# A hybrid decoder step on one core: the attention's masked products move to VectorE, the gate projection's pieces and the sample's state units change places, and one normalisation starts a piece later

## The chip, the cores and the metric

The kernel runs on one core of one Trainium2 chip. The metric is the device time of one execution in microseconds (us), as the median of several runs. TensorE (PE in the profile) multiplies matrices, VectorE (DVE), ScalarE (ACT) and GpSimd (POOL) do elementwise work, and SyncE (SP) issues the DMAs. Each engine works through its own queue in order; the engines wait for each other by semaphores. TensorE writes its results to PSUM, which this kernel uses as eight banks of 512 float32 values per partition. All operands of GpSimd in this kernel are in SBUF.

## The reference

One layer of a decoder is computed for a prompt of 1024 tokens and a sample group of 8 sequences of 4 tokens, in float32, with a width of 1024:

```
h = RMSNorm(x);  proj = h @ w_in
z | x,B,C | dt | q | k | v = split(proj)
y_ssd = RMSNorm( (SSD scan of silu(conv4(x,B,C)), dt) * silu(z) )      # 8 heads x 64, state 128, chunks of 128
y_att = sliding-window attention(q, k, v), window 128                  # 8 heads x 64, 2 kv heads, sinks, ALiBi
x = x + concat(y_ssd, y_att) @ w_out
h = RMSNorm(x);  u = conv3(h @ w_up);  x = x + (silu(u_gate) * u_val) @ w_down
```

The outputs are both groups' x, the last states of the scan and of the two convolutions, and the last keys and values.

## The kernel before, in words

The 1056 tokens (1024 of the prompt, then 32 of the sample) lie along the free dimension, features on the partitions. A float32 product is made of three passes: each operand is split into a rounded high part and a remainder, and `dense` (L147) issues high x high, high x low and low x high for each block of 128 inputs.

**Attention** (`att_unit`, L495 to L531) runs once for each of 8 query blocks and 2 halves of the heads, 16 times. TensorE makes the scores (L503), `probs` turns them into probabilities on VectorE, ScalarE and GpSimd, and TensorE transposes these into one PSUM bank `pt` (L517). The window of a block covers two key blocks, and the probabilities of both are held in one matrix: the entries on one side of the diagonal belong to the block's own keys, the others to the block before. So ScalarE copies the whole transposed matrix to SBUF (L519, `pt_[:, 1]`), GpSimd multiplies that copy by the triangle `tri` (L520, `pt_[:, 0]`), and TensorE multiplies both with values (L525): the masked part with the difference of the two value blocks (`vdif`), the whole with the values of the block before (`vall`). ScalarE copies the result out (`ya`, L530), and a DMA stores it to `yatt`.

**The state stage** follows a list of steps, `PLAN`. Each step issues the instructions of one piece:

- `uGT` is `ssd_unit`: the state unit of head group G (0 or 1) and token block T (0 to 7; 8 is the sample). It transposes its operands into a `px` bank (L611), scales them on GpSimd (`xd`, L618, L619), multiplies in banks `yy` (L653, L655), and updates the state that the next unit carries on, through the only bank of tag `st` (L660, L667). Decay rows are broadcast by DMA (`ab<-acd`, `Cs<-ead`). The sample's unit keeps its own result in the bank of tag `st` (L673, L684), loads four pieces of the old state (`h0`, `h<-in_h0T` in the profile), and makes masks and products on GpSimd (`cm`, L676; L643).
- `x0M` is `xbc`: one of the eight 128-wide chunks of the x,B,C projection with its convolution (L261 to L275).
- `zGI` is `z_block`: the gate projection of group G for token block I of the three blocks 0 to 384, 384 to 768 and 768 to 1056, that is 2 x 24 matmuls of 384 or 288 columns, and its silu (L708 to L710).
- `nGI` is `gate_norm`, the gated norm of a block (L719 to L739); `a0I` loads a block of the attention's output and splits it into the output projection's operands; `sGI` splits the state stage's result the same way.
- `oMQ` is `out_piece`: 24 matmuls for 128 output features M and quarter Q of the tokens (264 columns). Quarters 0 and 1 need token blocks 0 and 1 alone.

The operands of the output projection reuse the memory of the operands x of the input projections, so they can be written when the last gate piece has read x.

**After the plan** the loop at L939 issues the pieces of quarters 0 and 1 that the plan left out, with `half_done` after each M, which squares the result and adds it to a sum (`ssum`, L846). `half_prep(0)` then makes the norm of the first half: sums over the partitions on TensorE (L851), a reciprocal root on VectorE, a broadcast on TensorE (L858), the scaled result (L870), and the operands of the up projection (L882 to L887). The loop at L945 issues the pieces of quarters 2 and 3, in the order M = 4, 5, 6, 7, 0, 1, 2, 3. The up projection (L988) follows in a seven-product scheme, and then the down projection (L147).

The order of the instructions on each engine is not the program's alone: the framework lays it out when the kernel is built, with the program's order as priority and by times that it estimates, and lets later work go ahead where earlier work is not ready by its estimate.

## Time and profile before

| | |
|---|---|
| median of 3 runs | 1208.59 us (1203.76 to 1208.68) |
| profiled execution | 1208.17 us, its span 1206.4 us |
| TensorE busy | 1161.6 us, 96% |
| VectorE busy | 866.0 us, 72% |
| ScalarE busy | 506.6 us, 42% |
| GpSimd busy | 345.7 us, 29% |
| mean granted clock of TensorE | 0.98 |

A row of the timeline gives the start in us from the span's start, the duration, the engine, the line, the operation with what it writes and reads, and in brackets how long the engine sat idle before it and what it waited for. A row of the table by stage gives the stretch, its length, the busy time of each engine with the number of instructions, the mean granted clock of TensorE (1.00 is full, the clock is at full or half), the share of the DMA engines and their rate. In the list of waits, `A <- B: us, times, longest` says that A waited for B.

### The profile page before, as it was taken

The page shows a single profiled execution, that of the slowest core. Times are in us where ns is not written, and L with a number is a line of the kernel's source. Part 1 is how long each engine was busy: PE and PEld are TensorE (multiplying, and loading weights), DVE is VectorE, ACT ScalarE, POOL GpSimd, SP SyncE. Part 2 cuts the span into 40 slices and gives each one's busy share as a digit, 9 for nine tenths or more (in the row PEclk, how much of TensorE's full clock was granted, in tenths as well). Part 3 has the DMA queues.
Part 4 walks back from the last instruction along what each step waited for, and adds up shares of the span by engine and source line. Part 5 has one row for each costly group of instructions (what it writes and reads, how often), then busy time and mean ns, then how long its engine had stood idle before and what let it go on. Part 6 is the DMA issues. An engine that isn't in the chain of part 4 may idle for free.

```text
span 1206.4 us, 22111 instructions
## 1 busy us (share of the span) xinstructions
PE 1161.6 (96%) x8614; PEld 1112.8 (92%) x8614; DVE 866.0 (72%) x1739; ACT 506.6 (42%) x992; POOL 345.7 (29%) x471
## 2 busy tenths in 40 slices
PE   7999999989989999888999999999999999999998
PEld 7998878869867999888999999999999999999998
DVE  7678857476686677897766676666666787777764
ACT  7444643444544344464545454545544322112110
POOL 0125445253444000044344343534343111001000
PEclk9999999999988899899999999999999999999999
DMA  8211112132645413113222222222222854323303
GB/s 291 63 62 57 36 32 75 29 84 79 184 144 164 169 71 131 43 54 106 87 75 81 80 72 80 72 80 71 89 72 89 336 174 145 121 89 119 102 9 145
DMA packets 52362, 122.53 MB, mean 102 GB/s; under 512 B 9233, under 2 KB 19985, under 8 KB 52241
## 3 DMA queue, kind: packets, MB, share of 16 engines
q1 hardware_dynamic: 52256, 121.12, 29.9%
q8 instruction: 67, 1.10, 0.4%
q14 instruction: 39, 0.31, 0.1%
HBM read 94.86 MB, written 27.26 MB: 101 GB/s over the span
## 4 chain that ended last, share of the span: by engine, by line
PE 82%; DVE 8%; DMA 5%; ACT 2%; issue 2%; POOL 1%; SPq 0%; POOLq 0%; DVEq 0%; ACTq 0%
PE ps L147 37%; PE ps L988 31%; PE ps L199 6%; DMA raw<-in_wup 2%; DVE au L935 1%; PE ps L525 1%; PE sc L503 1%; PE yy L653 1%; DVE x2l L883 1%; PE ps L517 1%; PE st L660 1%; DMA Cs<-ead 1%; DVE c L1030 1%; DMA xr<-in_xT 1%; PE ps L339 0%
## 5 line engine op out<-in xcount | busy, mean ns | idle before, releaser
L988 PE MATMUL ps<-x2h,au 128*128 128x264 f32 x2464 | 456.4, 286 | 10.6 <-ACT x2h L882 4.0
L988 PEld LDWEIGHTS ps<-x2h,au 128*128 128x128 f32 x2464 | 384.0, 189 | 13.2 <-ACT x2h L882 4.4
L988 PE MATMUL ps<-x2l,au 128*128 128x264 f32 x1232 | 348.8, 285 | 0.4 <-DVE x2l L883 0.4
L988 PEld LDWEIGHTS ps<-x2l,au 128*128 128x128 f32 x1232 | 232.5, 189 | 0.8 <-DVE x2l L883 0.8
L1103 DVE TENSOR_TENSOR acc<-acc,ps 128x352 f32<-128x352 f32 x264 | 131.1, 517 | 65.3 <-PE ps L147 64.7
L147 PE MATMUL ps<-xh,uh 128*128 128x264 f32 (+3 forms) x528 | 163.8, 318 | 10.1 <-ACT xh L182 5.6
L147 PE MATMUL ps<-gh,ul 128*128 128x352 f32 x528 | 170.1, 322 | 0.0
L147 PE MATMUL ps<-gl,uh 128*128 128x352 f32 x528 | 170.0, 322 | 0.0
L147 PE MATMUL ps<-gh,uh 128*128 128x352 f32 x528 | 167.9, 322 | 0.6 <-ACT gh L179 0.6
L147 PE MATMUL ps<-xl,uh 128*128 128x264 f32 (+3 forms) x528 | 166.2, 315 | 0.3 <-DVE xl L183 0.3
L147 PE MATMUL ps<-xh,ul 128*128 128x264 f32 (+3 forms) x528 | 165.4, 313 | 0.0
L116 ACT ACTIVATE uh<-raw 128x1024 fp32r<-128x1024 f32 (+3 forms) x59 | 55.9, 953 | 194.1 <-PE ps L147 173.7
L1030 DVE SCALAR_TENSOR_TENSOR c<-u,colt,c 128x1072 f32<-128x1072 f32 x88 | 119.9, 1364 | 3.6 <-ACT c L1028 3.5
L147 PEld LDWEIGHTS ps<-xh,uh 128*128 128x128 f32 x528 | 101.5, 195 | 14.5 <-ACT xh L182 6.6
L935 DVE TENSOR_TENSOR au<-raw,au 128x512 fp32r<-128x512 f32 x115 | 78.7, 700 | 39.9 <-ACT au L934 39.8
L147 PEld LDWEIGHTS ps<-xl,uh 128*128 128x128 f32 x528 | 102.8, 195 | 1.8 <-DVE xl L183 0.8
L147 PEld LDWEIGHTS ps<-xh,ul 128*128 128x128 f32 x528 | 102.8, 195 | 1.8 <-issue 1.0
L147 PEld LDWEIGHTS ps<-gh,uh 128*128 128x128 f32 x528 | 98.8, 188 | 0.9 <-ACT gh L179 0.9
L147 PEld LDWEIGHTS ps<-gl,uh 128*128 128x128 f32 x528 | 99.2, 188 | 0.4
L147 PEld LDWEIGHTS ps<-gh,ul 128*128 128x128 f32 x528 | 99.3, 188 | 0.0
L934 ACT ACTIVATE au<-raw 128x512 fp32r<-128x512 f32 x115 | 71.2, 625 | 34.8 <-PE ps L147 9.0
L935 DVE TENSOR_TENSOR au<-t,au 128x512 fp32r<-128x512 f32 x46 | 41.6, 904 | 36.0 <-PE ps L988 18.9
(295 smaller groups left out, 1936.8 us busy)
## 6 DMA issues: line engine op xcount, KB each, us to landing
raw<-in_wup SPq DMA_DIRECT2D x46, 512.0 KB, 3.6
gr<-gd SPq DMA_DIRECT2D x22, 528.0 KB, 4.8
gd<-c SPq DMA_DIRECT2D x22, 512.0 KB, 2.6
raw<-in_wdn SPq DMA_DIRECT2D x22, 512.0 KB, 4.1
raw<-in_wout SPq DMA_DIRECT2D x12, 512.0 KB, 3.5
acc<-in_xT SPq DMA_DIRECT2D x16, 264.0 KB, 5.3
accd<-acc SPq DMA_DIRECT2D x16, 264.0 KB, 2.1
acc<-accd SPq DMA_DIRECT2D x8, 528.0 KB, 8.2
```

Of the source, the lines that this page charges most:

```text
L116: act.activation(out=hi, in_=raw, func=AF.Copy)
L147: pe.matmul(out=ps, lhsT=w(a, k), rhs=x(b, k), start=first and k == ks[0] and i == 0, stop=last and k == ks[-1] and i == 2)
L199: pe.matmul(out=ps[:m, :n], lhsT=x[k][c][:, a:a + m], rhs=w[k // nk][b][:, o:o + n], start=k == 0 and i == 0, stop=k == 7 and i == 2)
L503: pe.matmul(out=sb[:, v, c].rearrange("p i k -> p (i k)"), lhsT=qT[a][r, c], rhs=kT[b][r, o:o + 256], start=i == 0, stop=i == 2)
L517: pe.transpose(out=pt[:, h], in_=P[:, h], identity=ident)
L525: pe.matmul(out=po[64 * v:64 * v + 64, 0:256].rearrange("p (c q) -> p c q", c=2), lhsT=(vall[:, t - i] if i or not t else vdif[:, t - 1])[ ...
L653: pe.matmul(out=o, lhsT=xw[:, c], rhs=M[:, 2 * i + h], start=True, stop=not off)
L934: act.activation(out=u[:, 0:512], in_=src, func=AF.Copy)
L935: dve.tensor_tensor(out=u[:, 512:1024], in0=src, in1=u[:, 0:512].bitcast(F32), op=ALU.subtract)
L988: pe.matmul(out=ps, lhsT=wgt[:, 512 * a + 128 * k:512 * a + 128 * k + 128], rhs=xx[b][:, k], start=opens and k == 0 and i == 0, stop=k == ...
L1030: dve.scalar_tensor_tensor(out=c[:, 0:n], in0=u[:, j:j + n], scalar=col(C_FW + 3 * m + j), in1=c[:, 0:n], op0=ALU.mult, op1=ALU.add)
L1103: dve.tensor_tensor(out=o, in0=o, in1=ps[:, :PC], op=ALU.add)
```

## The change

It has three parts.

1. The masked product of an attention block (L520) runs on VectorE, and reads the transposed probabilities in PSUM in place of ScalarE's copy in SBUF.
2. `PLAN` is another order of the same steps. The sample's unit u08 comes after u11 and no longer after u04; z11 and z12 come between u10, u11, u08 and u12 and no longer ahead of u10; u18 comes after o21 near the end and no longer after n02; n02, s02, s11, s01 and the output pieces among them change places.
3. `half_prep(0)` is issued after the first piece of the second half (M = 4, quarter 2) and no longer ahead of it.

```
-PLAN = """u00 x07 u01 z00 u02 x06 x05 u03 u04 u08 u05 z01 u06 z10 u07 n00 z02 n01 z11 z12 u10 u11 u12 a00 u13 s00 n10 u14 s10 n02 u18 s02 u15 o20 o10 n11 s11 a01 u16 a02 o00 o30 u17 n12 s01 o21 o31 s12"""
+PLAN = """u00 x07 u01 z00 u02 x06 x05 u03 u04 u05 z01 u06 z10 u07 n00 z02 n01 u10 z11 u11 u08 z12 u12 a00 u13 s00 n10 u14 n02 s10 u15 o20 s02 n11 o10 a01 u16 s11 s01 o00 u17 a02 o30 o21 u18 n12 o31 s12"""
...
             pt_ = p.tile([128, 2, 4, 128], F32, tag="pt", name="pt", bufs=2)
             act.activation(out=pt_[:, 1], in_=pt, func=AF.Copy)
-            pool.tensor_tensor(out=pt_[:, 0], in0=pt_[:, 1], in1=b3(tri.unsqueeze(1), 128, 4, 128), op=ALU.mult)
+            dve.tensor_tensor(out=pt_[:, 0], in0=pt, in1=b3(tri.unsqueeze(1), 128, 4, 128), op=ALU.mult)
...
         half_done(m, 0, m == 0)
-    half_prep(0)
     for i, m in enumerate((4, 5, 6, 7, 0, 1, 2, 3)):
         if i >= 4:
             w[m] = None
         for q in (2, 3):
             out_piece(m, q)
+            if i == 0 and q == 2:
+                half_prep(0)
         half_done(m, 1, i == 0)
```

## The prediction

> **What bounds the kernel now.** I read the busy shares first, then the chain that ended last, then a table of busy times by stage, and only then the waits inside the stages that the change touches.

> ```profile
> span 1206.4 us, 22111 instructions
> PE 1161.6 (96%) x8614; PEld 1112.8 (92%) x8614; DVE 866.0 (72%) x1739; ACT 506.6 (42%) x992; POOL 345.7 (29%) x471
> PE 82%; DVE 8%; DMA 5%; ACT 2%; issue 2%; POOL 1%; SPq 0%; POOLq 0%; DVEq 0%; ACTq 0%
> ...
> core 0: us, PE busy (x) PEld busy (x) DVE busy (x) ACT busy (x) POOL busy (x), PEclk, DMA share, GB/s
> 105.00:265.00 160.00, 153.88 (x1123) 132.72 (x1125) 107.84 (x338) 75.61 (x226) 70.19 (x85) 0.98 0.16 47
> 265.00:329.50 64.50, 61.47 (x438) 54.06 (x434) 46.00 (x104) 36.04 (x87) 25.51 (x38) 0.95 0.44 133
> 329.50:403.50 74.00, 64.47 (x443) 53.09 (x443) 59.60 (x167) 31.07 (x77) 29.52 (x41) 0.82 0.49 146
> 403.50:430.70 27.20, 25.21 (x211) 25.00 (x212) 12.56 (x22) 7.26 (x11) 0.00 (x0) 1.00 0.47 163
> 430.70:478.00 47.30, 47.30 (x392) 47.30 (x392) 40.94 (x78) 20.73 (x33) 0.40 (x4) 1.00 0.27 97
> 478.00:572.50 94.50, 83.50 (x649) 80.60 (x647) 78.28 (x129) 48.98 (x87) 26.72 (x35) 0.96 0.21 73
> 572.50:945.00 372.50, 372.50 (x3053) 372.50 (x3054) 250.23 (x381) 187.22 (x328) 150.58 (x215) 1.00 0.25 83
> ```

> TensorE bounds the whole. From 572.50 us on it has no idle time, so whatever is won or lost before arrives at the end in full. What an edit can win is TensorE idle time and a low granted clock. The stages are attention (105 to 265), the first state units with gate pieces beside them (265 to 329.5), the later state units with output pieces (329.5 to 403.5), the rest of the first half's output pieces (to 430.7) and the second half's (to 478). The third is the poorest: 74.00 - 64.47 = 9.5 us idle, and a mean clock of 0.82, which costs up to 0.18 x 74 = 13.3 us, 22.9 us in all. Attention has 160.00 - 153.88 = 6.1 us idle.

> **Part 1, the masked product.** Removed are 16 products on POOL, each behind ACT's copy of the transposed probabilities; added are 16 on VectorE that read the same PSUM bank.

> ```profile
> L520 POOL TENSOR_TENSOR pt<-pt,cs x16: 1260/1290/2364, 108.7 to 262.1; 128x512 f32<-128x512 f32 x16
> ...
> PE ps L525 <- POOL pt L520: 3.1, 3, 2.1
> PE ps L147 <- DVE u L261: 1.8, 2, 1.5
> ...
> 162.91 1.08 PE L525 MATMUL ps<-pt,vdif 128*64 128x256 f32 x4 [2.08 <-POOL pt L520]
> ...
> L180 DVE TENSOR_TENSOR kTl<-ps,kTh x3: 173/677/684, 80.1 to 81.7; 128x512 fp32r<-128x512 f32 x2, 128x32 fp32r<-128x32 f32 x1
> ...
> 60.41 0.23 DVE L363 SCALAR_TENSOR_TENSOR dtr<-ps,rstd,rowt 128x8 f32<-128x8 f32 x1 [2.71 <-ACT vall L362]
> ```

> The trace has no such product on VectorE. The nearest row is L180: one operand from PSUM, one from SBUF, 512 columns, 0.68 us. So VectorE takes 16 x 0.68 = 10.9 us more, 107.84 to 118.7 us in 160. L363 shows that VectorE waits for ACT's last read of a PSUM tile, though it reads nothing that ACT wrote, so I let the product start after ACT's copy, as POOL's did. A block's latency then falls by 1.29 - 0.68 = 0.6 us, not by the whole 1.29. [...]

> Only three of the sixteen products kept TensorE waiting (3.1 us); the others are covered by projection matmuls of L147. At 162.91 0.6 of the 2.08 us goes, of the second (3.1 - 2.08 - 0.55) its 0.5. The third, the last block, is worth most:

> ```profile
> 259.72 2.41 POOL L119 TENSOR_TENSOR ul<-raw,uh 128x1024 fp32r<-128x1024 f32 x1
> 262.09 2.31 POOL L520 TENSOR_TENSOR pt<-pt,cs 128x512 f32<-128x512 f32 x1
> ...
> 261.34 5.58 DVE L270 SCALAR_TENSOR_TENSOR c<-u,chalf,c 128x1080 f32<-128x1080 f32 x3 [2.00 <-ACT c L267]
> ...
> 264.45 0.65 PE L525 MATMUL ps<-pt,vdif 128*64 128x256 f32 x4 [0.55 <-POOL pt L520]
> ...
> 268.57 1.17 PE L638 MATMUL px<-fm 128*128 128x128 f32 x4 [1.69 <-ACT xt L614]
> 270.89 1.22 PE L660 MATMUL st<-xd,xt 128*128 128x256 f32 x2 [1.15 <-POOL xd L619]
> ```

> The product waits on POOL behind a weight split and ends at 264.40, while VectorE idles for 2 us until 261.34. On VectorE it can end near 261, three microseconds earlier, and the output copy, its DMA and the first state unit behind them follow. The 0.55 goes, of the next two gaps (2.84 us) I take half, 1.4, and half of the clock loss in 265 to 329.5 (0.05 x 64.5 = 3.2), 1.6. Against that stands VectorE's longer queue (the convolution of L261 and L270 is behind it, and TensorE waits for L261 already 1.8 us): +0.6. Sum: -0.6 - 0.5 - 0.55 - 1.4 - 1.6 + 0.6 = **-4**. Ends: -11 (the 3.1 and 2.84 us and all clock loss of both stages, 0.02 x 160 + 3.2, with a little over for VectorE), and +2 (three exposed products each behind one L270, 1.3 us, in place of the 0.6 won).

> **Part 2, the order of the steps.** No work is added. The sample's unit of the first group (u08) goes from after u04 to after u11, past five units; that of the second (u18) from after u14 to after u17, past three; z11 and z12 go between u10, u11, u08 and u12; the splits s11 and s01 go ahead of o00.

> ```profile
> 329.50:354.00 24.50, 19.49 (x132) 15.06 (x134) 22.13 (x50) 13.16 (x36) 11.20 (x14) 0.79 0.54 157
> 354.00:382.00 28.00, 26.22 (x187) 20.87 (x181) 20.97 (x63) 11.22 (x28) 11.99 (x20) 0.82 0.42 118
> 389.50:402.50 13.00, 10.26 (x62) 9.30 (x61) 10.78 (x37) 4.47 (x7) 0.61 (x1) 0.74 0.41 151
> 300.00:321.00 21.00, 21.00 (x147) 17.79 (x146) 12.64 (x30) 9.37 (x24) 8.86 (x14) 1.00 0.66 208
> ...
> 307.03 0.65 PE L673 MATMUL yy<-xd,ab 32*128 32x64 f32 x4
> ...
> 323.80 0.68 PE L660 MATMUL st<-xd,xt 128*128 128x256 f32 x2
> ...
> 1133.70 22.97 PE ps L147 x144
> ...
> h<-in_h0T SPq DMA_DIRECT2D x16, 256.0 KB, 4.2
> Cs<-ead SPq DMA_DIRECT2D x14, 256.0 KB, 3.6
> ```

> Four terms. (i) 389.5 to 402.5 is the end of the plan, where o21 waits for the last splits: 13.00 - 10.26 = 2.7 us idle and 0.26 x 13 = 3.4 of clock. With s01 early, o21, o31 and ten more output pieces that need no third block can run beside u18 and the last norm. A piece is 24 matmuls of the 392 that took 47.30 us, so 2.9 us, and ten are 29 us of cover. Two thirds of 6.1: -4. (ii) 354 to 382 is u18 now: 1.8 idle and 0.18 x 28 = 5.0 of clock. At the end it has that cover: -4. Here the clock falls while TensorE is busy 26.22 of 28 us, with 32-wide matmuls (L673, L684). [...] (iii) u08 sits now at 300 to 321, where TensorE has 21.00 of 21 us of work at full clock, so it costs nothing. In its new place z12 covers it. A 352-column matmul takes 22.97 / 144 = 0.16 us, so z12's 48 of 288 columns are 6.3 us and z11's of 384 are 8.4 us. I give it most of what u18 costs where it is now: +5. (iv) z11 and z12 leave 303 to 328 and come in among u10 to u12, where 329.5 to 354 loses 5.0 idle and 0.21 x 24.5 = 5.1 of clock; two units are done sooner: -2. Sum: **-5**.

> Every instruction of u08 and u18 moves with them: per unit four loads of 256 KB on SP (4.2 us each to landing), two stores and a broadcast, and on POOL three copies, two scalings, the mask and four products. On SP u08's now stand behind the broadcasts of u05 to u11 (3.6 us each) and ahead of those of u12, u18's behind the loads of a01 and a02 and the weights of o00 to o21; I cost that at nothing, since two buffers of each let the loads run ahead, and in (iii) where they do not. Output pieces wait for x to be free, that is for z12: the attention load a00 and its POOL splits come after it as before. Ends of the part: -22.9, the stage's whole loss, and +15.5, priced below.

> **Part 3, the norm sums one piece later.**

> ```profile
> 429.60 0.55 PE L851 MATMUL ps<-ones,ssum 128*88 128x1 f32 x5 [1.99 <-DVE ssum L846]
> ...
> 478.18 0.43 DVE L777 TENSOR_TENSOR acc<-acc,ps 128x264 f32<-128x264 f32 x1 [2.51 <-PE ps L147]
> ```

> The 1.99 us in which TensorE waits for the sum are filled by o42 (2.9 us): **-2**. The normalisation on VectorE begins 2.9 - 2.0 = 0.9 us later while the pieces end 2 us earlier. VectorE idles 2.5 us before the last piece's addition, so its work still ends in time. Late next is the second half's normalisation, which follows the last piece and moves with it. Ends: -2 and +1.

> **Sum**: 1208.2 us, the time of the profiled execution (span 1206.4), - 4 - 5 - 2 = 1197. The three runs shown have a median 0.4 us above it, 1208.59, and one of 1203.76; I let 1197 stand against either.

> **Rivals.** *The state bank (slower).* u08 holds the single bank of tag st, in which each unit makes its state update, from 307.03 until the next update at 323.80: 16.8 us, in which no following unit can hand on its state. Now z02, z11 and z12 fill that. After u11 only z12 is sure, 6.3 us, so 10.5 us lie open, with the clock loss of u18's window, 5.0, beside them, and the output pieces start later, so that (i), (ii) and (iv) do not come: part 2 is +15.5 and the time 1208.2 - 4 - 2 + 15.5 = 1218. It decides for slower when over 7 us of the hold lie open. For it: 329.5 to 354 has VectorE at 22.13 of 24.50 already. Against: a unit's y needs the state before, not the bank, so u12, its norm and the first output pieces can run in the hold. 14%. *No change.* The product is hidden anyway, as thirteen of sixteen are; u08 inherits what u18 paid; only part 3 comes: 1206. For it: TensorE is 96% busy. Against: the idle time at the plan's end has a cause that the order removes. 24%. *More.* Dense pieces beside all units keep the clock up and three quarters of the 22.9 us go, -17: 1208.2 - 4 - 17 - 2 = 1185. For it: 300 to 321, the same kind of unit with dense pieces beside it, runs at clock 1.00. Against: the dense work is the same in total. 12%. My forecast, 1190 to 1203, has the other 50%.

> **Numbers.** About 0.5%, 6 us, is what a measurement of this kernel can tell from no change. Faster: 0.50 + 0.12, less a little for the forecast's upper edge, 0.60; slower 0.14; the rest 0.26. The range leaves out the deepest gain and the worst of the state bank: 1184 to 1212; the forecast's own is 1190 to 1203.

> **What would show it.** Part 1: a product row on VectorE near 0.68 us, behind ACT's copy; no wait of L525 for POOL; state units from 262 us on. Part 2: clock over 0.9 between the plan's gate pieces and its end, no idle time before the last o21 piece; wrong if the next state update after u08 comes over 10 us late with TensorE idle. Part 3: L851 without idle time ahead of it, and the products of the up projection starting 2 us nearer to it. The instruction order of each engine is laid out by a planner from estimated times; if it places far more than the edited steps otherwise, the sum by terms is void.

## The result, and the profile after

The changed kernel takes 1192.66 us (median of 6 runs, 1190.98 to 1195.53) against 1206.97 us (6 runs): ratio 0.9888, 95% interval 0.9871 to 0.9905, or 14.3 us less. The prediction said 1197.0 in 1184 to 1212. The profiled execution took 1193.78 us. Medians and ratios here and below leave out three executions with a low granted clock: one of the kernel before, one of h4_last, and the profiled one of f1_mask_head, whose mean clock was 0.535 over a span of 2168.7 us, so its trace is not used.

First the page's busy line, then the busy times by stage; the stages are those of the prediction's table, moved to where the matching work now stands. The new order also moves work between them: the second row has 486 matmuls for 438 before, the third 387 for 443.

```profile
span 1192.0 us, 22098 instructions
PE 1150.6 (97%) x8614; PEld 1108.3 (93%) x8614; DVE 872.0 (73%) x1755; ACT 504.7 (42%) x992; POOL 316.6 (27%) x455
PE 86%; DVE 9%; ACT 2%; issue 2%; DMA 1%; POOL 0%; SPq 0%; ACTq 0%; DVEq 0%
```

```profile
core 0: us, PE busy (x) PEld busy (x) DVE busy (x) ACT busy (x) POOL busy (x), PEclk, DMA share, GB/s
105.00:263.20 158.20, 155.02 (x1134) 134.12 (x1135) 112.30 (x355) 75.87 (x227) 44.44 (x70) 0.99 0.15 47
263.20:330.80 67.60, 65.20 (x486) 58.85 (x486) 52.93 (x125) 37.83 (x93) 27.77 (x42) 0.95 0.43 134
330.80:391.50 60.70, 48.43 (x387) 41.23 (x387) 50.77 (x144) 27.93 (x70) 25.79 (x36) 0.94 0.51 168
391.50:417.00 25.50, 25.50 (x211) 25.29 (x211) 12.06 (x24) 6.98 (x11) 0.00 (x0) 1.00 0.50 167
417.00:464.00 47.00, 47.00 (x394) 47.00 (x393) 37.77 (x73) 19.66 (x31) 0.40 (x4) 1.00 0.26 92
```

The one line to see is TensorE's busy time. The same 8614 matmuls took 1161.6 us before and take 1150.6 now: 11.0 of the span's 14.4 us are matmuls that run faster, and only 3.4 are idle time (1206.4 - 1161.6 = 44.8 before, 41.4 now). In the stage with the late state units, the clock was 0.82 and is 0.94, while TensorE idles longer there than before: 60.70 - 48.43 = 12.3 us, where 329.50 to 403.50 had 9.5. In these two traces the change won clock more than idle time.

That holds over all runs, not only in this trace. Each run lists its span and its mean granted clock; clock times span is called its time at full clock here, and the rest is what the clock took. The means over the runs, each ratio against the runs of the kernel before that were made beside it:

| kernel | parts in it | median us | ratio, 95% interval | at full clock | lost to the clock |
|---|---|---|---|---|---|
| before (86 runs) | none | 1207.0 | 1 | 1181.6 | 23.5 |
| changed | all three | 1192.7 | 0.9888 [0.9871, 0.9905] | 1180.1 | 10.9 |
| e1_mask | mask product | 1205.0 | 0.9981 [0.9963, 0.9999] | 1182.0 | 21.3 |
| e2_plan | order | 1209.4 | 1.0029 [1.0011, 1.0047] | 1184.1 | 24.3 |
| e3_norm | norm sums | 1204.3 | 0.9974 [0.9961, 0.9988] | 1181.9 | 20.0 |
| e4_mask_plan | mask, order | 1196.0 | 0.9908 [0.9889, 0.9927] | 1179.3 | 14.7 |
| f1_mask_head | mask, order up to u14 | 1200.8 | 0.9949 [0.9934, 0.9965] | 1179.1 | 20.4 |
| f2_mask_tail | mask, order from u14 | 1205.4 | 0.9988 [0.9973, 1.0003] | 1184.4 | 18.9 |
| h1_last_plan | last product, order | 1210.0 | 1.0031 [1.0006, 1.0057] | 1184.9 | 23.0 |
| h2_g0_plan | group 0's products, order | 1204.9 | 0.9990 [0.9974, 1.0006] | 1180.6 | 22.8 |
| h4_last | last product | 1207.5 | 0.9994 [0.9974, 1.0014] | 1181.2 | 23.1 |
| g2b_bank | mask, order, other bank | 1207.9 | 1.0014 [1.0001, 1.0027] | 1185.0 | 21.0 |
| f4_copy_plan | mask from SBUF, order | 1193.7 | 0.9898 [0.9878, 0.9919] | 1178.6 | 13.5 |
| h3_after_copy | all three, mask from SBUF | 1189.0 | 0.9856 [0.9834, 0.9878] | 1178.4 | 9.2 |

The last two columns add up to the span, which is 1.8 us short of the time. Their standard errors are 0.2 and 0.4 us for the kernel before, 0.4 to 1.1 and 0.6 to 2.0 for the others. By this split 12.6 of the changed kernel's 14.3 us are clock and 1.5 time at full clock. The two parts are not independent: over the 86 runs of the kernel before, an execution that lost 1 us more to the clock had 0.47 us less time at full clock (a fitted line), so it took only 0.53 us longer. The split says where the time stands, not what each us of clock is worth. A single execution of the kernel before scatters by 3.8 us (standard deviation) in what the clock takes, so a single trace says little about differences of 3 us; what follows leans on medians, and on traces for where things stand.

### The profile page after: what moved, and what is told of

Same layout as the page of the kernel before. It is cut to its first block, busy times and chain, and to the rows that moved or that the text cites. A ratio compares the mean times of both kernels' runs of the same rounds, so it can differ in the third digit from the quotient of the medians.

```text
span 1192.0 us, 22098 instructions
## 1 busy us (share of the span) xinstructions
PE 1150.6 (97%) x8614; PEld 1108.3 (93%) x8614; DVE 872.0 (73%) x1755; ACT 504.7 (42%) x992; POOL 316.6 (27%) x455
## 4 chain that ended last, share of the span: by engine, by line
PE 86%; DVE 9%; ACT 2%; issue 2%; DMA 1%; POOL 0%; SPq 0%; ACTq 0%; DVEq 0%
PE ps L147 39%; PE ps L989 32%; PE ps L199 6%; PE ps L525 1%; PE sc L503 1%; DVE au L935 1%; DVE x2l L883 1%; PE two L147 1%; DVE c L1031 1%; DMA raw<-in_wup 1%; PE ps L517 1%; PE yy L653 1%; PE st L660 0%; DMA gr<-gd 0%; PE px L611 0%
## 5 line engine op out<-in xcount | busy, mean ns | idle before, releaser
L147 PE MATMUL ps<-xh,uh 128*128 128x264 f32 (+3 forms) x528 | 164.1, 317 | 8.8 <-ACT xh L182 5.8
L147 PE MATMUL ps<-gh,ul 128*128 128x352 f32 x528 | 170.1, 322 | 0.0
L147 PE MATMUL ps<-gl,uh 128*128 128x352 f32 x528 | 170.0, 322 | 0.0
L147 PE MATMUL ps<-gh,uh 128*128 128x352 f32 x528 | 167.9, 322 | 1.1 <-ACT gh L179 1.1
L147 PE MATMUL ps<-xl,uh 128*128 128x264 f32 (+3 forms) x528 | 165.6, 314 | 0.0
L147 PE MATMUL ps<-xh,ul 128*128 128x264 f32 (+3 forms) x528 | 165.1, 313 | 0.0
L147 PEld LDWEIGHTS ps<-xh,uh 128*128 128x128 f32 x528 | 101.3, 193 | 12.6 <-ACT xh L182 5.8
L147 PEld LDWEIGHTS ps<-xl,uh 128*128 128x128 f32 x528 | 102.1, 193 | 1.8 <-POOL xl L180 0.4
L147 PEld LDWEIGHTS ps<-xh,ul 128*128 128x128 f32 x528 | 102.1, 193 | 1.5 <-issue 0.8
L147 PEld LDWEIGHTS ps<-gh,uh 128*128 128x128 f32 x528 | 98.8, 188 | 1.3 <-ACT gh L179 1.3
L147 PEld LDWEIGHTS ps<-gl,uh 128*128 128x128 f32 x528 | 99.2, 188 | 0.4
L147 PEld LDWEIGHTS ps<-gh,ul 128*128 128x128 f32 x528 | 99.3, 188 | 0.0
L119 DVE TENSOR_TENSOR ul<-raw,uh 128x1024 fp32r<-128x1024 f32 (+3 forms) x51 | 62.3, 1231 | 10.8 <-ACT uh L116 10.8
```

The costliest lines, as they stand in the source:

```text
L119: (e or dve).tensor_tensor(out=lo[:, i:i + n], in0=raw[:, i:i + n], in1=hi[:, i:i + n].bitcast(F32), op=ALU.subtract)
L147: pe.matmul(out=ps, lhsT=w(a, k), rhs=x(b, k), start=first and k == ks[0] and i == 0, stop=last and k == ks[-1] and i == 2)
```

## The experiments

**One part at a time.** e1_mask has the product on VectorE and nothing else, e2_plan the new PLAN alone, e3_norm the moved call of half_prep alone, e4_mask_plan the first two.

```
e1, e4:  -pool.tensor_tensor(out=pt_[:, 0], in0=pt_[:, 1], ...)
         +dve.tensor_tensor(out=pt_[:, 0], in0=pt, ...)
e2, e4:  -PLAN = """... u04 u08 u05 ... z11 z12 u10 u11 u12 ... u14 s10 n02 u18 s02 ...
         +PLAN = """... u04 u05 ... u10 z11 u11 u08 z12 u12 ... u17 a02 o30 o21 u18 ...
e3:      -half_prep(0) ahead of the loop
         +half_prep(0) after o42
```

> Part 1 alone: the masked product on VectorE, the plan and the place of the norm as before. Theory A (the prediction's terms add up: each part takes away a wait of its own): -4 us against the kernel before, ratio about 0.997; the last L525 about 7 us earlier than at 265.16 as in the changed kernel, of which some 3 us arrive at the first state unit. Rival B (the parts only pay together: the new plan is fitted to the block's new latency, and the planner's order of fillers moves): 0 to +3 us, ratio 1.000 to 1.003. Rival C (the plan carries nearly all): 0 us.

> Part 2 alone: the new order of steps, the product still on GpSimd. Theory A: the changed kernel is 14 us faster, 2 of them from part 3 and 4 from part 1, so -8 us, ratio 0.993; granted clock of 0.94 between the last gate piece and the end of the plan as in the changed kernel, in place of 0.82. Rival B: -4 us or less, ratio over 0.997. Rival C: -12 us, ratio 0.990.

> Part 3 alone: the first half's norm sums after piece o42. Theory A: -2.0 us, ratio 0.9983, L851 with no idle time before it, the first product of the up projection 2 us earlier and the wait at the second half's norm (498 to 503 us before) as long as it was. Rival: VectorE is late by 0.9 us more and gives part of it back there: -1 us.

> Parts 1 and 2, without part 3. Theory A: 2 us slower than the changed kernel, -12 us against before, ratio 0.990, and equal to the sum of the runs of part 1 alone and part 2 alone within 2 us. Rival B: much more than that sum, by 5 us or over. Rival C: equal to part 2 alone.

Against 1207.0 the mask alone gives -2, the norm sums alone -2.7, the order alone +2.4 with an interval that excludes a gain, and mask and order together -11. The terms do not add: the mask and the order sum to about 0, and 11 us come only when both are there. Rival B's reading (they pay together) stands, though its 0 to +3 us for the mask alone was not met; Theory A and Rival C fall. The norm sums add up by the time, 1196.0 - 1192.7 = 3.3 us on top of the two; how they do is taken up further below.

The profiled executions of the order alone (span 1209.3 us) and of mask and order (1195.3 us) differ by 14.0 us. Half of that, 7.0 us, lies at the end of the plan; 3.3 are won before the first state unit (266.56 and 263.24 us) and the rest in smaller parts. The first row is the order alone, the second mask and order, both the stretch between the second sample unit and the last o21; the matmul count is the same.

```profile
388.20:409.00 20.80, 17.23 (x99) 16.04 (x97) 15.39 (x41) 8.84 (x14) 0.00 (x0) 0.76 0.52 178
```

```profile
383.20:397.00 13.80, 12.50 (x99) 11.80 (x98) 11.50 (x33) 6.63 (x10) 0.00 (x0) 1.00 0.66 226
```

The same 99 matmuls take 20.80 us at clock 0.76 or 13.80 at 1.00, with 3.6 and 1.3 us idle. The 5.0 us of clock in this are one execution's: the changed kernel, with the same new order, has 0.87 at this place in its trace (further below). The chain of TensorE's waits in these parts (371 to 410 and 366.8 to 400 us):

```profile
PE ps L147 <- ACT xh L179: 1.5, 1, 1.5
PE ps L147 <- ACT uh L116: 0.7, 1, 0.7
PE ps L147 <- DVE xl L180: 0.5, 1, 0.5
PE ps L147 <- DVE ul L119: 0.5, 1, 0.5
PE nb L737 <- DVE yms L140: 0.3, 1, 0.3
```

```profile
PE ps L147 <- ACT xh L179: 1.3, 1, 1.3
```

With the order alone TensorE waits for splits of x and of the output weights four times close together; with the mask too, once.

**Head or tail of the order.** Both runs have the mask product on VectorE. f1_mask_head takes the new order up to u14, f2_mask_tail from there on.

```
f1:  ... u04 u05 z01 ... u10 z11 u11 u08 z12 u12 ... | u14 s10 n02 u18 s02 u15 ... (old)
f2:  ... u04 u08 u05 ... z11 z12 u10 u11 u12 ... (old) | u14 n02 s10 u15 ... o21 u18 n12 o31 s12
```

> The mask on VectorE, and of the new order only its head (z11 and z12 between u10 and u12, u08 after u11); from u14 on the old order, with u18 after s10 and the early splits late. Measured so far: mask alone 1205.0, mask with the whole new order 1196.0 us. Theory A (the tail, u18 last and the splits ahead, carries what the order saves once the mask is on VectorE; the head only costs u08's hold of the state bank): no gain from the head, 1204 to 1209, and the next state update after the group's last stands still behind u18. Rival B (the head carries it: the state units of the first group come sooner): 1197 to 1201. Rival C (only the whole order pays, since the planner lays out each half badly): 1203 to 1208 here and in the run with the tail alone.

> The mask on VectorE, the old head (u08 after u04, z11 and z12 ahead of u10), and the new tail (n02 ahead of s10, s11 and s01 ahead of o00, u18 last). Theory A (the tail carries the gain): 1193 to 1198, at or below the 1196.0 of mask with the whole new order, since u08 holds the state bank at a place where other work fills it. Rival B (the head carries it): 1202 to 1206, the mask alone being 1205.0. Rival C (only the whole pays): 1203 to 1208.

On top of the mask's 1205.0 the head gives -4.2, the tail +0.4, both -9.0. The head wins 2.9 us at full clock (1182.0 to 1179.1); the tail by itself loses 2.4 there. After the head the tail costs nothing at full clock (1179.3) and takes 5.7 us off the clock's loss. So Rival B's ranges were met (Rival C's only in f2), Theory A falls, and the tail pays only behind the new head.

**Is it the last block's late product?** In the prediction the last of the sixteen products carried most of part 1. h4_last moves only that one, h1_last_plan the same under the new order; every other instruction keeps its place on its engine. h2_g0_plan moves the eight of group 0 and leaves the last one on POOL.

```
+dv = g == 1 and t == 7          (h1, h4)      +dv = g == 0          (h2)
+(dve if dv else pool).tensor_tensor(out=pt_[:, 0], in0=pt if dv else pt_[:, 1], ...)
```

> The new order with only the last of the sixteen masked products (group 1, query block 7) on VectorE, the other fifteen on POOL as before. The order of the instructions on TensorE, ScalarE and SyncE is that of the new order alone (1209.4 us); only this product changes its queue. Theory A (the new order alone loses because the last product waits on POOL behind a weight split, which makes the first state unit 3 us late, and that alone undoes what the order saves): 1198 to 1203. Rival B (the late product is worth its own delay and no more): 1206 to 1208. Rival C (the gain of both parts together comes from where the planner puts the instructions once it counts the products on VectorE): 1206 to 1210, the state stage unchanged.

> The new order with the eight masked products of group 0 on VectorE and the eight of group 1, the late last one among them, on POOL. The planner then lays out the state stage nearly as with all sixteen on VectorE (the state updates stand at the same places among the gate projection's matmuls up to the tenth). Theory A (the last product's lateness undoes the gain): 1205 to 1210. Rival B (a product is worth its delay): about 1208. Rival C (the layout carries it): 1195 to 1200, with the first half's output pieces ending below 419 us.

> The kernel before with only the last masked product on VectorE; the order of every other instruction is unchanged. Theory A (most of what the mask is worth is the last block, as the prediction put it: its gap, half of the next two, and half of the clock loss behind them): 1204 to 1206, as the mask alone, the first state unit 2 to 3 us sooner. Rival B (it is the other fifteen, or the layout that follows from them): 1206 to 1208, that is nothing that can be told from the 1207.0 of before.

Under the new order Theory A falls: 1210.0 us where it said 1198 to 1203, beside 1209.4 with no product moved. Under the old order nothing can be told (1207.5 against 1207.2 beside it): the interval, 0.9974 to 1.0014, leaves room for a gain of 3 us and so for Theory A's 1204 to 1206. The timeline decides more. First h1_last_plan, below it the rows of e2_plan.

```profile
260.36 0.69 DVE L520 TENSOR_TENSOR pt<-ps,cs 128x512 f32<-128x512 f32 x1 [0.82 <-ACT pt L519]
264.03 0.65 PE L525 MATMUL ps<-pt,vdif 128*64 128x256 f32 x4
265.58 0.87 PE L611 MATMUL px<-idt,fm 128*128 128x128 f32 x6
```

```profile
265.01 0.65 PE L525 MATMUL ps<-pt,vdif 128*64 128x256 f32 x4 [0.55 <-POOL pt L520]
266.56 0.87 PE L611 MATMUL px<-idt,fm 128*128 128x128 f32 x6
```

The product ends at 261.05, as the prediction had it, but TensorE reaches its user only at 264.03, without waiting: other matmuls stand ahead of it in TensorE's order. h4_last shows the same under the old order; its rows, and below them the one of the kernel before that goes with the prediction's:

```profile
256.15 0.60 PE L517 MATMUL ps<-idt,s 128*128 128x128 f32 x4
257.76 0.69 DVE L520 TENSOR_TENSOR pt<-ps,cs 128x512 f32<-128x512 f32 x1 [0.82 <-ACT pt L519]
261.43 0.65 PE L525 MATMUL ps<-pt,vdif 128*64 128x256 f32 x4
265.29 0.87 PE L638 MATMUL px<-fm 128*128 128x128 f32 x4 [1.43 <-ACT xt L614]
267.87 1.22 PE L660 MATMUL st<-xd,xt 128*128 128x256 f32 x2 [1.72 <-POOL xd L619]
```

```profile
258.55 0.60 PE L517 MATMUL ps<-idt,s 128*128 128x128 f32 x4
```

From the transposes (L517) to the product's user (L525) TensorE needs 261.43 - 256.15 = 5.28 us, before 264.45 - 258.55 = 5.90. So the earlier product is worth 0.6 us to TensorE and not three, and the two gaps behind it are 1.43 + 1.72 = 3.15 us where they were 2.84. (The state units start at 262.98 in this trace, 3.0 us sooner than before; 1.7 of that is one half-rate stretch less ahead of them.) With all sixteen on VectorE the planner draws the attention's products forward (the last L525 of the changed kernel starts at 257.9 us):

```profile
L525 PE MATMUL ps<-pt,vall x64: 379/379/430, 112.1 to 257.9; 128*64 128x256 f32 x64
```

With group 0 alone the state units are laid out almost as in e4_mask_plan, and full-clock time drops to 1180.6. But the clock still takes 22.8 us, and between 386 and 404 us, at the plan's end, TensorE still waits for a split (first row). Its last product is not late, though it is still on POOL (the rows below): the planner has put POOL's weight split behind it, it ends at 259.53, and TensorE takes it up at 261.70 without waiting.

```profile
PE ps L147 <- ACT uh L116: 2.9, 1, 2.9
```

```profile
258.25 1.28 POOL L520 TENSOR_TENSOR pt<-pt,cs 128x512 f32<-128x512 f32 x1 [5.42 <-ACT pt L519]
261.70 0.65 PE L525 MATMUL ps<-pt,vdif 128*64 128x256 f32 x4
262.79 2.40 POOL L119 TENSOR_TENSOR ul<-raw,uh 128x1024 fp32r<-128x1024 f32 x1
```

At 1204.9 us it is 4.5 us below the order alone, and still above Rival C's 1195 to 1200. Theory A's number (1205 to 1210) is nearly met, but its reason, a late last product, is absent; so this run does not test it. With h1, though, the delay of the last product is excluded as the cause of the 11 us, and h4's rows say why. What is left is the order that the planner makes when it counts all sixteen on VectorE, together with the latency of the other fifteen. These two could not be separated, since any other subset moves the order as well; that the differing waits are for splits over 100 us behind the products speaks for the order, but it is an argument and no run shows it alone.

**Does u08's hold of the state bank cost?** g2b_bank puts the sample units' y and its transpose into tag nb, under mask and order.

```
-yy = psd.tile([128, 512], F32, tag="st" if smp else "yy", name="yy")
+yy = psd.tile([128, 512], F32, tag="nb" if smp else "yy", name="yy")
-ps = psd.tile([128, 512], F32, tag="st", name="yt")
+ps = psd.tile([128, 512], F32, tag="nb", name="yt")
```

> Mask on VectorE and the new order (1196.0 us), and the sample units' y and its transpose in the bank of tag nb, so that u08 no longer holds the single bank of tag st. Theory A (u08's hold, 13.8 us from its first product to the next state update with some 4.6 us of it idle, is what the new order still pays): 1191 to 1194, the next state update within 8 us of the one before. Rival B (the hold is covered, the idle time there comes from VectorE's queue): 1195 to 1197. Rival C (the norm's sums, which use nb, now wait for the sample units): 1197 to 1202.

It is 12 us slower than e4_mask_plan, outside all three. The hold did not cost what Theory A said: with the bank free the next state update after u08's first product at 327 comes at 339.25 (first row), in the changed kernel at 340.93 (the rows below it).

```profile
339.25 0.70 PE L660 MATMUL st<-xd,xt 128*128 128x256 f32 x2
```

```profile
327.16 0.88 PE L673 MATMUL yy<-xd,ab 32*128 32x64 f32 x6
339.68 0.41 PE L691 MATMUL yt<-idt,ys 128*128 128x128 f32 x2 [0.71 <-DVE ys L688]
340.93 0.67 PE L660 MATMUL st<-xd,xt 128*128 128x256 f32 x2 [0.51 <-DVE fm L698]
```

TensorE's longest waits in g2b_bank, from 326 to 424 us, show what came in its place:

```profile
PE px L611 <- DVE cb L640: 3.1, 1, 3.1
PE nb L737 <- DVE yms L140: 2.6, 2, 1.4
PE ps L147 <- DVE ul L119: 1.6, 1, 1.6
```

The long gap for cb stays (3.4 us in the changed kernel), so it comes from VectorE, which in the changed kernel is busy for all of 331.29 to 334.70, and not from the bank. The norm's L737 in nb now waits 2.6 us where it did not wait in e4_mask_plan, but for VectorE's `yms`, not for the sample unit; the wait for the bank that Rival C named is seen only the other way round, with 0.4 us before the sample unit's L673. The planner has put that second sample unit behind the norm, at 385 us where it was at 368. Since the order moved too, the 12 us are not the price of the bank alone.

**Where the product reads from.** f4_copy_plan (on e4_mask_plan) and h3_after_copy (on the changed kernel) read ScalarE's copy in SBUF; all engines keep their order.

```
-dve.tensor_tensor(out=pt_[:, 0], in0=pt, ...)
+dve.tensor_tensor(out=pt_[:, 0], in0=pt_[:, 1], ...)
```

> Mask on VectorE and the new order, as in the run of both (1196.0 us), but VectorE's product reads the copy that ScalarE has made in SBUF, not the PSUM bank. The instructions stand in the same order on every engine. Theory A (the product waits for ScalarE's read of the bank in any case, so where its operand lies is nothing): 1195 to 1197, the product's row 0.6 to 0.75 us. Rival B (two SBUF operands make VectorE share with POOL, as other such products show 0.16 us alone and 0.93 beside a POOL operation): the row is uneven, some of the sixteen over 1 us, and the time 1197 to 1201.

> The changed kernel whole, with its masked product on VectorE reading ScalarE's copy in SBUF in place of the PSUM bank; the instructions stand in the same order on every engine. In the run with the first two parts the same edit gave 1193.7 against 1196.0 us, which their intervals do not tell apart. Theory A (where the operand lies changes nothing, since the product waits for ScalarE in any case and the row was 0.68 us there as well or near it): 1191 to 1194, with the 1192.7 of the changed kernel inside. Rival B (a product that reads SBUF is shorter or frees the PSUM bank sooner, and the 2.3 us repeat): 1189 to 1191, faster than both kernels. By the split of each run into its time at full clock and what the clock took, mean granted clock times span: A 1179 to 1181 at full clock, 10 to 13 lost.

The first row is the changed kernel's product, the second h3_after_copy's (shortest, median and longest duration in ns).

```profile
L520 DVE TENSOR_TENSOR pt<-ps,cs x16: 678/692/692, 108.3 to 253.6; 128x512 f32<-128x512 f32 x16
```

```profile
L520 DVE TENSOR_TENSOR pt<-pt,cs x16: 678/692/1829, 107.7 to 252.4; 128x512 f32<-128x512 f32 x16
```

Both times are lower, by 2.3 and 3.6 us, but neither pair's intervals part (0.9889 to 0.9927 and 0.9878 to 0.9919; 0.9871 to 0.9905 and 0.9834 to 0.9878). h3_after_copy's 1189.0 us (4 runs) is the lowest of all and below both kernels; that it beats the kernel before is shown, that it beats the changed one is likely and not shown. The row is no shorter, and one product of the sixteen takes 1.83 us: it starts 1.11 us into a weight split of POOL (L119), and outlasts it. Operations of POOL that start while such a product runs are longer too: L325 takes 0.57 us for 0.20 in the changed kernel, L492 1.53 to 1.55 for 1.04. In the changed kernel, with the operand in PSUM, a product also starts 1.11 us into a split of L119 (243.68 in 242.57 to 244.96 us) and takes 0.69 us. VectorE's L138, with its operands in SBUF, is longer beside POOL too: in the kernel before it takes 0.11 to 0.17 us in 48 of its 60 places (0.16 at 297.47, POOL idle), and 0.39 to 1.21 us in the twelve where an operation of POOL is running when it starts (0.93 at 327.54, beside L180). So in these rows, with both operands in SBUF, the one that comes second takes longer, and the saving, if it is one, isn't in the product itself. What carries it stays open.

## Why the prediction was right, and where it was not

The sum of -11 came close to -14.3, with the right sign. That it came so close is luck: parts 1 and 2 by themselves give -2 and +2.4 where -4 and -5 were forecast, and their 11 us come from the two together, which no term of the sum stands for. Single-trace figures below carry the scatter named above. The rows of the changed kernel that answer to the four terms of part 2:

```profile
263.10:328.00 64.90, 62.50 (x467) 56.97 (x466) 50.98 (x124) 35.03 (x87) 24.97 (x39) 0.95 0.40 125
328.00:366.80 38.80, 27.80 (x237) 22.20 (x237) 35.55 (x83) 22.23 (x59) 20.10 (x29) 0.96 0.49 162
366.80:383.40 16.60, 16.17 (x127) 13.77 (x125) 10.38 (x41) 4.91 (x12) 8.50 (x11) 1.00 0.67 210
383.40:397.00 13.60, 12.77 (x90) 12.53 (x91) 10.20 (x30) 5.93 (x9) 0.00 (x0) 0.87 0.58 199
```

- **Part 1, -4; alone it gave -2.** What the signs said is there: the product's row is 0.69 us for 0.68, it follows ACT's copy (all sixteen start after the copy has ended, ten of them 0.03 us after; VectorE idled for it 7.6 us in five places), L525 no longer waits for POOL (of its 3.1 us one wait of 1.4 us is left, for VectorE's product), and the state units begin at 263.10 for the 262 named, 266.01 before. The step that failed is that a last product three microseconds earlier brings the state units forward by as much. By h4_last it is worth 0.6 us to TensorE; the 2.9 us come when the planner, with all sixteen on VectorE, orders TensorE anew (263.13 in e1_mask as well).
- **Part 2, -5; alone it gave +2.4, with part 1 about -9.** The failing step is the sum itself: it took the parts as independent. The prediction's own caveat, that a planner lays out the order and may void the terms, is what happened. Term by term, in the presence of part 1:
  - (i) the plan's end: 0.8 us idle and 0.13 x 13.6 = 1.8 of clock, for 2.7 and 3.4; 3.5 us won where 4 were forecast. In e2_plan, without the mask, the same place lost 3.6 and 5.0. One wait of 1.3 us for a split (L179, at 384.23) is left there, so the idle time that the prediction's sign named is smaller and not gone.
  - (ii) u18's window: 0.4 us idle and clock 1.00, for 1.8 and 5.0; 6.4 won, 4 forecast.
  - (iii) and (iv): up to 366.80 TensorE idles 2.4 + 11.0 = 13.4 us and the clock takes 3.2 + 1.6 = 4.8, 18.2 in all. Before, 265 to 354 lost 8.0 idle and 8.3 clock, 16.3. So the first group's price came: about 5 us more idle time, 3.5 less lost to the clock, +1.9 net, where (iii) and (iv) with part 1's three microseconds there gave 0.
- **Part 3, -2; alone -2.7, on top of the others -3.3.** The wait went as forecast: L851 has no idle time ahead of it, and in e3_norm the time from the last piece of the first half to the first product of the up projection is 48.1 us for 50.4. The term is not the whole account, though. In the means the time at full clock did not fall (1181.6 to 1181.9 alone, 1179.3 to 1180.1 on top of the others); the gain stands on the clock's side (23.5 to 20.0, 14.7 to 10.9). The traces show a part of both. In eight of the ten without part 3 half rate follows between L851 and the up projection and takes 1.7 to 3.4 us, in none of the three with it. And some idle time comes back: in the 95 us from the up projection's first product TensorE idles 10.4 to 10.6 us with part 3, and without it 9.7 in the mean (8.9 to 11.0).

```profile
419.93 0.28 PE L147 MATMUL ps<-xh,uh 128*128 128x264 f32 x1
420.04 1.03 PE L851 MATMUL ps<-ones,ssum 128*88 128x1 f32 x12
```

- **The state bank rival** did not come. u08 holds the bank for 340.93 - 327.16 = 13.8 us, over the ten that were to mark it, but only 3.4 + 0.7 + 0.5 = 4.6 of these are idle, below the 7 that decide; and g2b_bank shows that freeing the bank doesn't bring the update forward by more than 2 us.

*Clock and idle time.* The prediction counted about 4 us of its 11 as clock (1.6 in part 1, the rest by the shares of idle time and clock in the rows of part 2); by the split above it is 12.6 of 14.3. It put the low clock of 354 to 382 down to 32-wide matmuls, in a stage where TensorE was busy for 26.22 of 28 us. The stretches below, first of the kernel before and then of the changed one, show that this was partly wrong: the half rate there follows a piece in which TensorE was busy for only 2.11 of 3.41 us. They are cut where the granted clock changes.

```profile
360.97:364.38 3.41, 2.11 (x14) 1.57 (x14) 2.35 (x8) 0.95 (x3) 2.32 (x5) 1.00 0.70 215
364.38:374.62 10.24, 10.24 (x47) 7.55 (x46) 6.68 (x19) 7.10 (x19) 4.57 (x6) 0.50 0.41 118
...
391.69:395.10 3.41, 1.51 (x12) 1.07 (x8) 3.20 (x9) 1.85 (x4) 0.00 (x0) 1.00 0.30 111
395.10:401.93 6.83, 6.83 (x34) 6.80 (x34) 5.58 (x21) 2.62 (x4) 0.00 (x0) 0.50 0.24 91
```

```profile
331.29:334.70 3.41, 0.45 (x4) 0.45 (x5) 3.41 (x4) 3.00 (x10) 1.62 (x3) 1.00 0.99 336
334.70:338.11 3.41, 3.41 (x19) 3.00 (x22) 2.17 (x5) 3.21 (x8) 0.00 (x0) 0.51 0.92 317
```

In these two traces the granted clock is 1.00 or 0.50, and half rate comes in stretches of one to three pieces of 3.41 us, up to 570 us eight before and six after. Thirteen of the fourteen follow a piece in which TensorE was partly idle (busy for at most 2.15 of the 3.41 us): after a piece with 1.51 of 3.41 us busy come 6.83 us at half rate. The fourteenth is taken up further below. The changed kernel idles 12.3 us in its late state units and pays half rate for two pieces there: one gap of 3.4 us falls almost whole into one piece, and of the gaps of 1.5 us and less only the one before the plan's end is followed by another (at 385.9, behind a piece 2.15 us busy). The rest leave their pieces over half busy. That such an order keeps the clock is in the means over all runs; why this order spreads its gaps that way was not taken apart further.

## What to carry to other kernels

Split each run's time into clock times span and the rest before explaining a difference: here TensorE's idle time changed little, and most of the gain was matmuls at full clock. The two parts move against each other, so the split shows where to look and proves no cause. Parts of a change that pass through one planner are not to be summed: each part's sign can turn with the other one present, so run each alone and together. A wait at the end of a chain is worth its length only if the engine that waits comes to it first in its own order; where other work stands ahead of it, taking the wait away yields little, here 0.6 us of three.

## What the hardware showed that was not expected

Seven of the 8 exceptions are one place, near 31 us:

```profile
31.20 1.99 PE L155 MATMUL ps<-ones,ssum 128*128 128x1 f32 x18
```

These 18 matmuls have one column each. In the changed kernel's trace all 1.99 us of them fall into one piece (30.95 to 34.37), which is followed by half rate (34.37 to 37.78), though TensorE counts as busy all through; without the one-column matmuls it would be busy for 1.65 us, less than half of the piece. In the kernel before the grid cuts them into 1.42 and 0.57 us, and no half rate follows. Of the thirteen traces eight have 1.92 us or more of them in one piece, and seven of these pieces are followed by half rate; in the other five, with at most 1.85 us in one piece, none is. The piece at 360.97, 62% busy, holds matmuls of 32 rows. That such narrow matmuls count for less than their time would fit this, but no run shows it by itself, and the rest of the exceptions are not explained.
